# Six gate units made in pairs by seven block products, in the state space projections' stage

## The chip, the cores and the metric

The kernel runs on one core of one Trainium2 chip. The metric is the device time of one execution in microseconds (us). A measurement is the median of three runs; the profile is one more execution, recorded by the hardware.

## The reference, cut to what matters

One decoder layer over 1024 tokens with 1024 channels, in float32. Three mixers read one input projection, and each one's output is weighted by gates from the same projection:

```python
h = rms_norm(x, pre_mix_norm)
proj = h @ w_in
z, xbc, dt_raw, sb_qkv, nsa_q, nsa_kv, nsa_gate, merge_gate = split(proj)
y_ssm = ssm_mixer(z, xbc, dt_raw, ...)
y_sb  = stick_breaking_attention(sb_qkv)
y_nsa = nsa_attention(nsa_q, nsa_kv, nsa_gate, ...)
gm = sigmoid(merge_gate).reshape(bsz, s, 3, D_MODEL)
mixed = gm[:, :, 0] * (y_ssm @ w_br_ssm) + gm[:, :, 1] * (y_sb @ w_br_sb) + gm[:, :, 2] * (y_nsa @ w_br_nsa)
x = x + rms_norm(mixed @ w_out, post_mix_norm)      # then a convolved, gated feed-forward layer

def stick_breaking_attention(q, k, v):              # 4 heads of 128; for each block of queries
    ls = log_sigmoid(q @ k.T * scale)
    lk = where(mask, ls - q @ k.T * scale, 0)
    later = cumsum(lk, reversed over the keys) - lk # a sum that runs from the last key to the first
    out = where(mask, exp(ls + later), 0) @ v
```

The merge gates are 3072 channels, 24 units of 128 channels. The change concerns six of these units.

## The kernel before, in words

Everything is held with channels on the partitions and tokens along the free dimension. A float32 operand of TensorE is split into a high part (a copy in a shorter format) and a low part (the difference), and a product is made as three matmuls, high x high, high x low and low x high, of 128 x 128 weights by 128 x 512 tokens.

**A unit** is 128 output channels for all 1024 tokens. Made directly (`fine_steps`, `half_unit`), it is two halves of 512 tokens, each of 8 steps of 3 matmuls: 48 matmuls. ScalarE makes the high part of the weights (`whi`, L287), GpSimd the low part (`wlo`, L292). A gate unit ends with `sigmoid` (L262 to L264: Exp, Ln, Exp on ScalarE) and a DMA to a scratch tensor `g_d` (L580).

**The state space projections' stage** (`ssm_units`, from about 65 to 330 us) makes 24 units in 12 pairs. A pair is a 2 x 2 block product (two units by two token halves, with the depth in two halves) made with seven block products in place of eight. `weights7` (L532 to L552) loads both units' weights, forms the sums of blocks on GpSimd and splits them; `product` issues the 12 matmuls of one block product; `snap` (L610) copies a partial sum out of PSUM on ScalarE, and VectorE combines. A convolution (L325 to L331) and Silu (L622) follow, in a table set of ScalarE of its own; Exp and Ln are in another, and the program switches between them with table loads. One gate unit (number 0) is made directly ahead of the pairs.

**The sparse attention's stage** (to about 800 us) takes gate units 1 to 11 as filling between its own matmuls.

**The stick-breaking attention's stage** (`sb_stage`, about 820 to 1145 us) goes over four heads. A head has two chains, `chain(h, 1, ...)` for the later 512 queries, with eight blocks of 128 keys, and `chain(h, 0, ...)` for the earlier 512, with four. Each block of keys is a round of three steps:
- `score`: three matmuls into a bank of `ps_s` (or `ps_t` for chain 0); then VectorE takes a minimum (L1196), ScalarE Exp and Ln (L1197, L1198) and a copy (L1200), VectorE a maximum (L1201) and on the diagonal a mask (L1185).
- `carry`: VectorE subtracts the running sum's row of the round before (L1211), ScalarE makes `s_hi` (L1214), GpSimd `s_lo` (L1215), and two matmuls with a triangle (`rtab`) follow in the same bank.
- `value`: VectorE adds the bank to the copy (L1223), ScalarE takes Exp (L1224) and `w_hi` (L1228), VectorE `w_lo` (L1229), and three matmuls with the values go to `ps_o` (or `ps_b`).

Two banks are there for `ps_s`, so a score two rounds on waits for the addition L1223 that empties its bank.

Between these steps `fill.take` hands out steps of filling, `SB_FILL` per step of a chain on average: first the projections of the next head (three direct units, 144 matmuls, and some transposes), then the gate units `SB_GATES[h]` to `SB_GATES[h+1]`. Heads 0, 1 and 2 have two gate units each, head 3 has four (18 to 21), and two more (22, 23) are held back behind the last head's end.

**What sets the order.** The order of the instructions of each engine is fixed when the program is built, by a list scheduler that takes an instruction from later in the program where the next one's operands aren't ready by its own clock (`schedule_with_timeline_sim=True`). In the sparse attention's stage TensorE keeps the written order. On the chip each engine works through its fixed list in order. Tiles of one pool are handed out in the written order, so a unit that waits for a buffer holds back the ones behind it.

Of the kernel before, what the change touches and what calls it, by code (L numbers as in the profile page):

```python
# [28 lines left out]
PV_PRE, PV_FFN, PV_SSM, PV_D, PV_CW, PV_CB, PV_FW, PV_FB, PV_PM, PV_PF = np.cumsum(  # L29
    [0, 8, 8, 8, 8, 64, 16, 132, 44, 8]).tolist()  # L30
# [139 lines left out]

START_GATES = 1
N_GATES = 12
SB_GATES = (12, 14, 16, 18, 22, 24)

SB_LATE = 24

# [4 lines left out]
NSA_LEAD = 0  # L181
NSA_SWITCH = (10, 1)
MM_LAG = 3
SB_FILL = (2.2, 2.2, 2.2, 2)

SSD_AT = (0, 1, 8, 9)

# [23 lines left out]
def trunk(ctx: ExitStack, tc: tile.TileContext, A: dict, outT: bass.AP, dbg=None):  # L211
    nc = tc.nc
    act = nc.scalar.activation
# [18 lines left out]
    TABLE = "natural_log_exp_and_others"  # L232
# [28 lines left out]
    def sigmoid(dst, src):  # L261
        act(dst, src, AF.Exp, scale=-1.0)  # L262
        act(dst, dst, AF.Ln, bias=1.0)
# [55 lines left out]
    def hs(h):  # L319
        return slice(h * 512, (h + 1) * 512)  # L320

    def conv(o, h, ps, taps, bias, halo):

        n = len(taps) - 1
        act(o, ps, AF.Identity, bias=bias, scale=taps[0])  # L325
        if h == 0:
            V.tensor_copy(halo[:, :n], ps[:, 512 - n:])
        for d in range(1, n + 1):
            V.scalar_tensor_tensor(o[:, d:], ps[:, :512 - d], taps[d], o[:, d:], op0=OP.mult, op1=OP.add)  # L329
            if h == 1:  # L330
                V.scalar_tensor_tensor(o[:, :d], halo[:, n - d:n], taps[d], o[:, :d], op0=OP.mult, op1=OP.add)  # L331
# [240 lines left out]

    gp = hx.enter_context(tc.tile_pool(name="gp", reuse_waits="tile", bufs=2))

    def gates(j0, j1, steps=unit_steps):
        for j in range(j0, j1):
            def evict(h, ps):
                e = gp.tile([128, 512], F32, name="gate_e")
                sigmoid(e, ps)
                nc.sync.dma_start(g_d[j * 128:(j + 1) * 128, hs(h)], e)  # L580
            yield from steps(U_GATE + j, evict)
# [4 lines left out]
    def ssm_units():  # L586


        wx = early.enter_context(tc.tile_pool(name="wx0", side="right", reuse_waits="tile", bufs=2))
        ev = early.enter_context(tc.tile_pool(name="ev", side="right", reuse_waits="tile", bufs=2))  # L590
        rhs = {q: [None] * 4 for q in range(1, 8)}
        for k in range(4):
            b = [xs[h][k + n] for n in (0, 4) for h in range(2)]
            combos(*b, V)
            for q, n, h in ((1, 0, 0), (2, 4, 0), (3, 4, 1)):
                rhs[q][k] = h_rhs(k + n, h)
            for q, t in zip((6, 5, 4, 7), b):
                rhs[q][k] = t
        for q in (6, 7, 5, 4):
            for k in range(4):  # L600
                t, hi, lo = rhs[q][k], x_t(), x_t()
                act(hi, t, AF.Copy)
                V.tensor_tensor(lo, t, fl(hi), op=OP.subtract)
                rhs[q][k] = hi, lo

        Fill(gates(0, START_GATES)).rest()

        def snap(ps):
            t = x_t(F32)
            act(t, ps, AF.Copy)  # L610
            return t

        for q, m in itertools.product(range(4), (0, 2, 1)):
            u0 = 6 * q + 2 * m
            halos = [ev.tile([128, 4], F32, name="halo", bufs=4) for _ in range(2)]

            def evict(n, h, ps):
                o = ev.tile([128, 512], F32, name="o")
                if m < 2:
                    cu = q * 4 + 2 * m + n  # L620
                    conv(o, h, ps, [pvc(PV_CW, 4 * cu + 3 - d) for d in range(4)], pvc(PV_CB, cu), halos[n])
                act(o, o if m < 2 else ps, AF.Silu)  # L622
                nc.sync.dma_start(s_d[(u0 + n) * 128:(u0 + n + 1) * 128, hs(h)], o)

            w = weights7(wx, A["wfm"][U_SSM + u0], A["wfm"][U_SSM + u0 + 1], 512)
            x, y, z, v = ps_d(), ps_s(), ps_t(), (ps_o, ps_b)[m % 2]()
            product(x, w, rhs, 1, True)
            s1 = snap(x)
            product(y, w, rhs, 2, True)
            V.tensor_tensor(y, y, s1, op=OP.add)  # L630
            evict(0, 0, y)
            product(x, w, rhs, 6, False)
            s2 = snap(x)
            product(z, w, rhs, 7, True)
            product(x, w, rhs, 5, False)
# [1275 lines left out]
```

## Time and profile before

| | |
|---|---|
| time, median of 3 runs | 2241.54 us (2239.26 to 2242.5) |
| the profiled execution, first to last instruction | 2244.0 us |
| TensorE busy | 2167.6 us, 97% of the span |
| VectorE, ScalarE, GpSimd busy | 1314.7, 1204.4, 1269.3 us |
| first and last carry of the longer chains, stick-breaking stage | 841.99 us and 1142.53 us |

The profiled execution has no other time of its own than this span, which is 2.5 us above the median. A matmul of 512 columns shows as 0.39 us, but matmuls overlap, and in an undisturbed stretch one starts every 0.22 us; time for TensorE is therefore counted below by starts. Below, "lost" is time in which TensorE starts nothing though the list has more.

### The profile page before, as it was taken

The numbers are of one execution on the slowest core, as the hardware profiler recorded it, in microseconds if no ns is written. First come the engines' busy times: TensorE is split into PE (matmuls) and PEld (weight loads), VectorE is DVE, ScalarE is ACT, GpSimd is POOL, SyncE is SP. The second block draws the span as 40 slices with busy tenths as digits, with TensorE's granted clock in tenths as the row PEclk, the third lists the DMA queues.
The fourth block names the chain that finished last, engine by engine and source line by source line (L and its number), as shares of the span: only waits on it lengthen the run. The fifth ranks groups of instructions, "written<-read, shape, count | busy, mean of one in ns | idle before, by whom it ended". The sixth has DMA issues, their size and how long they took to land.

```text
span 2244.0 us, 30112 instructions
## 1 busy us (share of the span) xinstructions
PE 2167.6 (97%) x10589; PEld 1731.7 (77%) x10589; DVE 1314.7 (59%) x2419; ACT 1204.4 (54%) x2240; POOL 1269.3 (57%) x1122
## 2 busy tenths in 40 slices
PE   7999999999999999999999999999999999999997
PEld 7888889876666688888776678888778888878887
DVE  6765545257557426556537662228955767675776
ACT  6544442467757746667755531236644444575534
POOL 3777641146746734333337646568686777765743
PEclk9999999999999999999999999999999999999999
DMA  5233341321221011112262264235332323255433
GB/s 174 82 113 108 113 134 55 111 84 35 55 75 34 13 57 41 64 59 88 99 216 87 81 219 141 88 128 184 116 99 80 118 94 113 99 187 175 141 104 118
DMA packets 120104, 234.64 MB, mean 105 GB/s; under 512 B 28816, under 2 KB 43088, under 8 KB 119952
## 3 DMA queue, kind: packets, MB, share of 16 engines
q1 hardware_dynamic: 117072, 230.13, 31.2%
q10 hardware_dynamic: 2880, 2.59, 0.3%
q8 instruction: 83, 1.36, 0.3%
q14 instruction: 69, 0.57, 0.1%
HBM read 169.10 MB, written 63.57 MB: 104 GB/s over the span
## 4 chain that ended last, share of the span: by engine, by line
PE 80%; DVE 6%; ACT 4%; POOL 3%; issue 3%; DMA 2%; SPq 0%; DVEq 0%; ACTq 0%; POOLq 0%
PE dense L219 55%; PE ps_s L219 7%; PE ps_o L219 7%; PE ps_t L219 6%; PE ps_b L219 4%; PE psn L219 3%; DVE u L329 1%; POOL wlo L292 1%; POOL wlo L538 0%; DMA wraw<-in_wfm 0%; ACT dec L1302 0%; ACT wT L1000 0%; DMA traw<-in_wtm 0%; POOL h_lo L472 0%; DVE x L1530 0%
## 5 line engine op out<-in xcount | busy, mean ns | idle before, releaser
L292 POOL TENSOR_TENSOR wlo<-wraw,whi 128x256 fp32r<-128x256 f32 x344 | 273.1, 825 | 274.3 <-ACT whi L287 274.1
L219 PE MATMUL dense<-h_hi,whi 128*128 128x512 f32 x656 | 262.6, 400 | 0.0
L219 PE MATMUL dense<-h_hi,wlo 128*128 128x512 f32 x656 | 256.7, 392 | 1.2 <-POOL wlo L538 1.2
L219 PE MATMUL dense<-h_lo,whi 128*128 128x512 f32 x656 | 256.5, 391 | 0.0
L1011 POOL TENSOR_TENSOR wT_lo<-wT,wT_hi 128x512 fp32r<-128x512 f32 x132 | 168.8, 1288 | 84.8 <-ACT wT_hi L1010 76.5
L219 PE MATMUL dense<-hi,whi 128*128 128x512 f32 x576 | 214.5, 391 | 1.3 <-ACT whi L287 1.3
L219 PE MATMUL dense<-hi,wlo 128*128 128x512 f32 x512 | 200.8, 394 | 0.5 <-POOL wlo L292 0.4
L219 PE MATMUL dense<-x,uhi 128*128 128x512 f32 x600 | 191.8, 392 | 2.7 <-ACT uhi L546 1.5
L219 PE MATMUL dense<-lo,whi 128*128 128x512 f32 x448 | 176.1, 393 | 0.0
L287 ACT ACTIVATE whi<-wraw 128x1024 fp32r<-128x1024 f32 (+1 forms) x94 | 92.6, 985 | 154.4 <-PE dense L219 125.3
L547 POOL TENSOR_TENSOR ulo<-uf,uhi 128x1024 fp32r<-128x1024 f32 x38 | 91.8, 2416 | 115.0 <-ACT uhi L546 109.6
L219 PEld LDWEIGHTS dense<-h_hi,wlo 128*128 128x128 f32 x656 | 123.1, 188 | 27.9 <-POOL wlo L538 1.6
L219 PEld LDWEIGHTS dense<-h_hi,whi 128*128 128x128 f32 x656 | 123.7, 189 | 23.4
L219 PEld LDWEIGHTS dense<-h_lo,whi 128*128 128x128 f32 x656 | 123.5, 188 | 22.7
L219 PEld LDWEIGHTS dense<-x,uhi 128*128 128x128 f32 x600 | 112.4, 188 | 28.4 <-ACT x L610 2.4
L1215 POOL TENSOR_TENSOR s_lo<-sa,s_hi 128x512 fp32r<-128x512 f32 (+2 forms) x48 | 53.7, 1119 | 139.7 <-ACT s_hi L1214 139.7
L219 PEld LDWEIGHTS dense<-hi,whi 128*128 128x128 f32 x576 | 108.4, 188 | 25.5 <-ACT whi L287 2.1
L972 DVE TENSOR_REDUCE mx<-ps_t 128x1 f32<-128x384 f32 (+3 forms) x192 | 98.7, 520 | 48.9 <-PE ps_t L219 46.0
L329 DVE SCALAR_TENSOR_TENSOR u<-dense,pv,u 128x511 f32<-128x511 f32 (+1 forms) x140 | 103.5, 741 | 34.5 <-ACT u L325 34.5
L219 PEld LDWEIGHTS dense<-hi,wlo 128*128 128x128 f32 x512 | 96.3, 188 | 23.7 <-POOL wlo L292 2.0
L550 POOL TENSOR_TENSOR ulo<-uf,uhi 128x1024 fp32r<-128x1024 f32 x38 | 91.8, 2415 | 39.6 <-ACT uhi L549 38.0
L538 POOL TENSOR_TENSOR wlo<-wraw,whi 128x1024 fp32r<-128x1024 f32 x38 | 92.8, 2441 | 30.2 <-ACT whi L537 30.1
(555 smaller groups left out, 6088.4 us busy)
## 6 DMA issues: line engine op xcount, KB each, us to landing
wraw<-in_wfm SPq DMA_DIRECT2D x62, 512.0 KB, 3.7
wraw<-in_wup SPq DMA_DIRECT2D x52, 512.0 KB, 3.5
lo<-m_d SPq DMA_DIRECT2D x58, 256.0 KB, 3.2
g_d<-gate_e SPq DMA_DIRECT2D x48, 256.0 KB, 2.0
s_d<-o SPq DMA_DIRECT2D x48, 256.0 KB, 2.0
ge<-g_d SPq DMA_DIRECT2D x24, 512.0 KB, 3.4
m_d<-u SPq DMA_DIRECT2D x44, 256.0 KB, 2.0
row<-s_d SPq DMA_DIRECT2D x16, 512.0 KB, 5.0
```

The source lines that it names most:

```text
L219: i = f(*a, **k)
L287: act(hi, raw, AF.Copy)
L292: (V if tiles else P).tensor_tensor(lo[:, s], raw[:, s], fl(hi[:, s]), op=OP.subtract)
L329: V.scalar_tensor_tensor(o[:, d:], ps[:, :512 - d], taps[d], o[:, d:], op0=OP.mult, op1=OP.add)
L538: P.tensor_tensor(wlo, raws[0], fl(whi), op=OP.subtract)
L547: P.tensor_tensor(l24, f24, fl(h24), op=OP.subtract)
L550: P.tensor_tensor(l31, f31, fl(h31), op=OP.subtract)
L972: V.tensor_reduce(mx[:, h, a, n:n + 1], pm[:, :w], axis=AX, op=OP.max)
L1011: P.tensor_tensor(lo, wf, fl(hi), op=OP.subtract)
L1215: (P if SB_SLO else V).tensor_tensor(s_lo[:, c0:], a[:, c0:], fl(s_hi[:, c0:]), op=OP.subtract)
```

## The change

Gate units 12 to 17 leave the filling of heads 0, 1 and 2 of the stick-breaking stage. They are made in the state space projections' stage as three pairs, by the same seven block products as the state space units, behind the last of those. The code of a pair becomes a function `pair(u, m, evict)`, and the end of a gate unit a function `gate_out`. The instruction that loads the table set with Exp and Ln is written a second time, between the state space pairs and the gate pairs. `SB_FILL`, the steps of filling per step of a chain, goes from 2.2 to 1.4 for heads 0 to 2, as the filling there goes from 80 to 48 steps a head. Heads 0 to 2 now have the next head's projections alone as filling; head 3 has its four gate units, and the two held back are as before.

```diff
 N_GATES = 12
-SB_GATES = (12, 14, 16, 18, 22, 24)
+PAIR_GATES = 12, 18
+SB_GATES = (18, 18, 18, 18, 22, 24)
...
-SB_FILL = (2.2, 2.2, 2.2, 2)
+SB_FILL = (1.4, 1.4, 1.4, 2)
...
+    def gate_out(j, h, ps):
+        e = gp.tile([128, 512], F32, name="gate_e")
+        sigmoid(e, ps)
+        nc.sync.dma_start(g_d[j * 128:(j + 1) * 128, hs(h)], e)
...
-        for q, m in itertools.product(range(4), (0, 2, 1)):
...
-            w = weights7(wx, A["wfm"][U_SSM + u0], A["wfm"][U_SSM + u0 + 1], 512)
+        def pair(u, m, evict):
+
+            w = weights7(wx, A["wfm"][u], A["wfm"][u + 1], 512)
             x, y, z, v = ps_d(), ps_s(), ps_t(), (ps_o, ps_b)[m % 2]()
             product(x, w, rhs, 1, True)
             s1 = snap(x)
...
+        for q, m in itertools.product(range(4), (0, 2, 1)):
...
+            pair(U_SSM + u0, m, evict)
+        tc.keep_in_program_order(nc.scalar.preload_act_table_set(TABLE))
+        for m, j in enumerate(range(*PAIR_GATES, 2)):
+            pair(U_GATE + j, m, lambda n, h, ps: gate_out(j + n, h, ps))
```

The rows below are from the lists that the scheduler made, one row an instruction: line, operation, output <- inputs, shape. Line numbers of the changed kernel are 1 to 25 higher than before (L220 for L219, L647 for L622).

**TensorE, the last head of the stick-breaking stage, chain 1.** `row` tiles are queries and keys, `s_hi` and `s_lo` the operands of a carry, `w_hi` and `w_lo` those of a value step, `dense` is filling. Before:

```order
L219 MATMUL ps_s<-row_10135,row_10137 128x512
L219 MATMUL ps_s<-s_hi,rtab 128x512
L219 MATMUL ps_s<-row_10136,row_10137 128x512
L219 MATMUL ps_s<-row_10135,row_10138 128x512
L219 MATMUL dense<-h_hi,whi 128x512
L219 MATMUL dense<-h_lo,whi 128x512
L219 MATMUL dense<-h_hi,wlo 128x512
L219 MATMUL ps_s<-s_lo,rtab 128x512
L219 MATMUL ps_t<-s_hi,rtab 128x384
```

And now:

```order
L220 MATMUL ps_s<-s_lo,rtab 128x512
L220 MATMUL ps_o<-w_hi,row_10295 128x384
L220 MATMUL ps_o<-w_hi,row_10296 128x384
L220 MATMUL ps_o<-w_lo,row_10295 128x384
L220 MATMUL ps_s<-row_10291,row_10293 128x512
L220 MATMUL ps_s<-row_10292,row_10293 128x512
L220 MATMUL ps_s<-row_10291,row_10294 128x512
L220 MATMUL ps_s<-s_hi,rtab 128x512
L220 MATMUL ps_s<-s_lo,rtab 128x512
L220 MATMUL ps_o<-w_hi,row_10295 128x512
```

Before, filling stands between the carries of this chain in all rounds but one; now the filling stands earlier in the list, and six rounds in a row of this head have none.

**TensorE, the end of chain 1 of the second head.** Before, the last rounds of it (`ps_o` with `row_8729`) have filling among them:

```order
L219 MATMUL ps_s<-s_lo,rtab 128x512
L219 MATMUL ps_s<-row_9430,row_9433 128x256
L219 MATMUL dense<-h_hi,whi 128x512
L219 MATMUL ps_o<-w_hi,row_8729 128x512
L219 MATMUL ps_o<-w_hi,row_8730 128x512
L219 MATMUL dense<-h_lo,whi 128x512
L219 MATMUL dense<-h_hi,wlo 128x512
L219 MATMUL ps_o<-w_lo,row_8729 128x512
```

And now (the same chain's `ps_o` has `row_9161`; `ps_t` is the next head's chain 0):

```order
L220 MATMUL ps_s<-row_9157,row_9160 128x512
L220 MATMUL ps_s<-s_hi,rtab 128x512
L220 MATMUL ps_o<-w_hi,row_9161 128x512
L220 MATMUL ps_o<-w_hi,row_9162 128x512
L220 MATMUL ps_s<-s_lo,rtab 128x512
L220 MATMUL ps_o<-w_lo,row_9161 128x512
L220 MATMUL ps_t<-s_hi,rtab 128x512
```

The gate units that stood between these rounds are gone, and the next head's projections stand ahead of them.

**ScalarE, the end of the state space units.** Before (`o` is the output of a state space unit, `thi` and `whi` belong to what follows):

```order
L622 ACTIVATE o<-o 128x512
L384 ACTIVATE thi<-traw 128x512 x2
L856 ACT_TABLE_LOAD
L856 ACTIVATE ea<-hv 128x16
L325 ACTIVATE o<-dense,pv 128x512
L622 ACT_TABLE_LOAD
```

And now (`uhi` are weights of the first gate pair):

```order
L647 ACTIVATE o<-o 128x512
L263 ACT_TABLE_LOAD
L263 ACTIVATE gate_e<-ps_s 128x512
L264 ACT_TABLE_LOAD
L264 ACTIVATE gate_e<-gate_e 128x512
L265 ACT_TABLE_LOAD
L265 ACTIVATE gate_e<-gate_e 128x512
L647 ACT_TABLE_LOAD
L647 ACTIVATE o<-o 128x512
L550 ACTIVATE uhi<-uf_2821 128x1024
```

The first gate half stands ahead of the last Silu: three loads for its three functions, one back to Silu's set, and one more behind it. From the first pair on there are five table loads here, where three were.

More of the change, by code (lines that the diff above doesn't have):

```diff
@@ L573, in trunk @@
     gp = hx.enter_context(tc.tile_pool(name="gp", reuse_waits="tile", bufs=2))
+    def gate_out(j, h, ps):
+        e = gp.tile([128, 512], F32, name="gate_e")
+        sigmoid(e, ps)
+        nc.sync.dma_start(g_d[j * 128:(j + 1) * 128, hs(h)], e)
     def gates(j0, j1, steps=unit_steps):
         for j in range(j0, j1):
[L577 to L581, printed above, removed]
+            yield from steps(U_GATE + j, lambda h, ps: gate_out(j, h, ps))
     s_d = scratch("s_d", [24 * 128, T])
@@ L611, in snap @@
             return t
-        for q, m in itertools.product(range(4), (0, 2, 1)):
[L614 to L623, printed above, removed]
-            w = weights7(wx, A["wfm"][U_SSM + u0], A["wfm"][U_SSM + u0 + 1], 512)
+        def pair(u, m, evict):
+            w = weights7(wx, A["wfm"][u], A["wfm"][u + 1], 512)
             x, y, z, v = ps_d(), ps_s(), ps_t(), (ps_o, ps_b)[m % 2]()
@@ L644, in ssm_units, with evict @@
             evict(0, 1, x)
+        for q, m in itertools.product(range(4), (0, 2, 1)):
+            u0 = 6 * q + 2 * m
+            halos = [ev.tile([128, 4], F32, name="halo", bufs=4) for _ in range(2)]
+            def evict(n, h, ps):
+                o = ev.tile([128, 512], F32, name="o")
+                if m < 2:
+                    cu = q * 4 + 2 * m + n
+                    conv(o, h, ps, [pvc(PV_CW, 4 * cu + 3 - d) for d in range(4)], pvc(PV_CB, cu), halos[n])
+                act(o, o if m < 2 else ps, AF.Silu)
+                nc.sync.dma_start(s_d[(u0 + n) * 128:(u0 + n + 1) * 128, hs(h)], o)
+            pair(U_SSM + u0, m, evict)
+        tc.keep_in_program_order(nc.scalar.preload_act_table_set(TABLE))
+        for m, j in enumerate(range(*PAIR_GATES, 2)):
+            pair(U_GATE + j, m, lambda n, h, ps: gate_out(j + n, h, ps))
     ssm_units()
-    tc.keep_in_program_order(nc.scalar.preload_act_table_set(TABLE))
     early.close()
```

## The prediction

> **What bounds the kernel now.** I read the page first: shares of the engines, and the chain that ended last.
>
> ```profile
> PE 2167.6 (97%) x10589; PEld 1731.7 (77%) x10589; DVE 1314.7 (59%) x2419; ACT 1204.4 (54%) x2240; POOL 1269.3 (57%) x1122
> PE 80%; DVE 6%; ACT 4%; POOL 3%; issue 3%; DMA 2%; SPq 0%; DVEq 0%; ACTq 0%; POOLq 0%
> ```
>
> TensorE (PE) bounds the whole, so a matmul less is worth its start interval, as long as the stage it leaves still keeps TensorE supplied. The interval comes from a stretch of the projections' stage, in the view by windows (length, then busy time and count of each engine, TensorE's clock, DMA):
>
> ```profile
> 120.00:140.00 20.00, 20.00 (x89) 16.39 (x88) 5.12 (x8) 8.06 (x12) 13.74 (x9) 1.00 0.43 145
> ```
>
> 89 matmuls in 20 us are 0.2247 us each. ScalarE is busy 8 and GpSimd 14 of the 20 us, so gate pairs have room there.
>
> The stage that gives the work up is different. Its longer chains are serial: each of 32 rounds needs the carry of the round before. In the timeline, the second matmul of a carry (start, duration) marks a round's end; here are the first of the 32, three near the end, and the last:
>
> ```profile
> 841.99 0.38 PE L219 MATMUL ps_s<-s_lo,rtab 128*128 128x256 f32 x1
> ...
> 1104.37 0.39 PE L219 MATMUL ps_s<-s_lo,rtab 128*128 128x512 f32 x1
> 1112.93 0.40 PE L219 MATMUL ps_s<-s_lo,rtab 128*128 128x512 f32 x1
> 1122.02 0.39 PE L219 MATMUL ps_s<-s_lo,rtab 128*128 128x512 f32 x1
> ...
> 1142.53 0.39 PE L219 MATMUL ps_s<-s_lo,rtab 128*128 128x512 f32 x1
> ```
>
> Counting TensorE's list between carries, a 512-wide matmul at 0.2247 us and a narrower one in proportion: the round to 1112.93 holds 8.37 us of matmuls and took 8.56, so it was bound by TensorE. The next holds no filling, 4.33 us of matmuls, and took 9.09: 4.8 us lost. All 31 intervals hold 283.8 us and took 300.5, so some 12 us more are lost in small pieces. The windows show the hole:
>
> ```profile
> 1110.00:1115.00 5.00, 4.34 (x21) 3.12 (x19) 4.65 (x9) 3.95 (x8) 2.42 (x2) 1.00 0.25 92
> 1115.00:1120.00 5.00, 3.26 (x14) 1.95 (x14) 4.33 (x9) 4.49 (x9) 0.16 (x1) 1.00 0.14 52
> ```
>
> **The change part by part.**
>
> *Matmuls.* Six direct units are 6 x 48 = 288; three pairs are 3 x 84 = 252. Saved: 36 x 0.2247 = 8.1 us. The stick-breaking stage gives up 64.7 us, the projections' stage gains 56.6.
>
> *The projections' stage.* Table loads on ScalarE rise from three to five in this place. Before, they stood with room around them:
>
> ```profile
> 321.25 1.28 ACT L856 ACT_TABLE_LOAD   x1
> 322.55 0.22 ACT L856 ACTIVATE ea<-hv 128x16 f32<-128x16 f32 x1
> 325.54 0.63 ACT L622 ACTIVATE o<-o 128x512 f32<-128x512 f32 x1 [0.68 <-DVE o L331]
> 295.12 1.06 ACT L546 ACTIVATE uhi<-uf 128x1024 fp32r<-128x1024 f32 x1 [0.38 <-PE dense L219]
> L262 ACT ACTIVATE gate_e<-dense x48: 576/587/601, 61.4 to 1155.9; 128x512 f32<-128x512 f32 x48
> L263 ACT ACTIVATE gate_e<-gate_e x48: 612/632/695, 62.1 to 1158.6; 128x512 f32<-128x512 f32 x48
> ```
>
> Now they are queued ahead of `uhi`, weights of the first gate pair, for which TensorE waits. After the pair's second block product ScalarE has: Exp 0.59, load 1.28, Ln 0.63, load 1.28, Exp 0.63, load 1.28, Silu 0.63, `uhi` 1.06 = 7.4 us, and an addition on VectorE ahead of it (0.69, below): 8.1. TensorE's list has 35 matmuls there, 7.9 us. So 0.2 us shows, 0.5 with the hand-overs; bounds 0, and 8.1 if none of that cover held. [...] Here the next instruction follows the load by 0.02 us, and the row decides.
>
> Of other waits, the snapshots' grow with three pairs more, and two gaps stand at the stage's end:
>
> ```profile
> PE dense L219 <- ACT x L610: 2.1, 4, 0.9
> 320.76 0.39 PE L219 MATMUL ps_t<-thi,h_hi 128*128 128x256 f32 x1 [0.59 <-ACT thi L384]
> 322.12 0.39 PE L219 MATMUL ps_t<-tlo,h_hi 128*128 128x256 f32 x1 [0.73 <-POOL tlo L385]
> ```
>
> 2.1 us over 12 pairs make 0.5 for three. The two gaps (1.3) may stay or go; I leave them. Projections' stage: +1.0 us. The sparse attention's list on TensorE is unchanged.
>
> *The stick-breaking stage.* Of its DMAs only the six units' weight loads and twelve stores go; they hid behind matmuls. What counts is the cover. In the changed list, rounds without filling (by the order, counted from 0) are 13 and 14 in the second head, with round 12 nearly bare, and 24 to 29 in the last head. Their matmuls: 5.56, 2.25, 1.80 = 9.6 us; and 2.36, 1.74, 2.19, 1.46, 1.63, 2.25 = 11.6 us. TensorE cannot run ahead, since its list is fixed and the next score waits for a bank. What does such a round cost? The trace has one link of it, from a score (PE) to the addition that frees a bank for the next:
>
> ```profile
> 1120.12 0.96 PE L219 MATMUL ps_s<-row,row 128*128 128x512 f32 x3
> 1121.19 0.69 DVE L1196 TENSOR_SCALAR sa<-ps_s 128x512 f32<-128x512 f32 x1 [0.52 <-PE ps_s L219]
> 1121.91 0.63 ACT L1197 ACTIVATE sa<-sa 128x512 f32<-128x512 f32 x1 [0.52 <-DVE sa L1196]
> 1122.52 0.60 ACT L1200 ACTIVATE sz<-ps_s 128x512 f32<-128x512 f32 x1
> 1123.01 0.62 ACT L1198 ACTIVATE sa<-sa 128x512 f32<-128x512 f32 x1
> 1123.66 0.69 DVE L1201 TENSOR_TENSOR sa<-ps_s,sa 128x512 f32<-128x512 f32 x1 [1.18 <-ACT sa L1198]
> 1124.46 0.68 DVE L1211 TENSOR_TENSOR sa<-sa,ps_s 1x512 f32<-1x512 f32 x1
> 1125.17 0.69 DVE L1223 TENSOR_TENSOR sz<-sz,ps_s 128x512 f32<-128x512 f32 x1
> ```
>
> 1125.86 - 1120.12 = 5.74 us. VectorE's changed list has these in this sequence in the bare rounds, so 5.74 is a round's period; the 9.09 is the upper bound, as in that round the shorter chain and a gate's sigmoid were in the way. Narrow rounds shrink as ScalarE's do:
>
> ```profile
> L1197 ACT ACTIVATE sa<-sa 128x512 f32<-128x512 f32 x24 | 15.1, 630 | 19.8 <-DVE sa L1196 19.8
> L1197 ACT ACTIVATE sa<-sa 128x384 f32<-128x384 f32 x8 | 4.2, 522 | 4.6 <-DVE sa L1196 4.5
> L1197 ACT ACTIVATE sa<-sa 128x256 f32<-128x256 f32 x16 | 6.7, 418 | 4.0 <-DVE sa L1196 4.0
> L1229 DVE TENSOR_TENSOR w_lo<-sz,w_hi 128x512 fp32r<-128x512 f32 x23 | 18.8, 820 | 21.4 <-ACT w_hi L1228 21.4
> ```
>
> By 522/630 and 418/630: 4.8 and 3.8 us. Second head: 3 x 5.74 - 9.6 = 7.6 lost. Last head: 2 x 3.8 + 4.8 + 3 x 5.74 = 29.6, less 11.6 = 18.0; the shorter chain's last four value steps share VectorE in rounds 24 to 26, about 4 us by their `w_lo`, additions and masks, of which I count half, 2. Together 27.6. Lost before and gone now: 4.8. Net +22.8. The floor is VectorE alone, 0.69 + 0.69 + 0.68 + 0.69 + 0.82 = 3.57 a wide round: 10.7 and 22.5 (with the narrow rounds in proportion at 2.4, 2.4 and 3.0, and the 4), so 1.1 + 10.9 lost, net +7.2. The ceiling is 9.09 a round, in proportion: 27.3 - 9.6 and 46.9 - 11.6, net +48.2.
>
> *The clock.* TensorE's clock drops after thin stretches:
>
> ```profile
> 524.00:526.00 2.00, 0.94 (x8) 0.40 (x7) 1.97 (x4) 1.25 (x3) 1.46 (x2) 1.00 0.27 74
> 526.00:528.00 2.00, 1.26 (x8) 0.50 (x7) 1.41 (x6) 0.63 (x1) 1.42 (x5) 1.00 0.00 0
> 528.00:530.00 2.00, 1.50 (x7) 1.21 (x8) 0.44 (x1) 0.24 (x1) 0.90 (x1) 0.62 0.02 4
> 530.00:532.00 2.00, 2.00 (x9) 1.39 (x7) 1.25 (x4) 1.25 (x3) 0.41 (x1) 0.53 0.15 45
> ```
>
> 2.2 us busy of 4 brought it to about half; 3.26 of 5 above did not. The bare rounds hold 39% (11.6 of 29.6). At half clock three score matmuls take 0.65 us more in a round's period: nine rounds 5.9, and one slow stretch of some 3.4 us behind each of two tails costs 1.7 each. Bounds 0 and 9.3; I take 4, since slow matmuls raise the busy share again. [...]
>
> *Sum:* -8.1 + 1.0 + 22.8 + 4 = +19.7 us: 2263.7 for the profile's 2244.0, and 2261 against the median 2241.54.
>
> **The rivals.**
> 1. *The saving stands*, because filling that moved ahead covers the 12 us of small losses elsewhere and bare rounds run at VectorE's floor: -8.1 + 1.0 + 7.2 - 12 = -11.9 at most, half of the 12 giving -5.9: 2236. For it: VectorE is the busiest engine in the hole. Against it: 5.74 had little beside it. Faster.
> 2. *Floor without that cover*: -8.1 + 1.0 + 7.2 = +0.1, 2242: no change.
> 3. *Bare rounds cost as the one of before did*, every engine's queue in the way: -8.1 + 1.0 + 48.2 + 4 = +45.1 at most; midway between the two periods, +32: 2274. For it: the only complete bare round measured. Against: no gates' sigmoids are left there in the second head.
> 4. *The table loads stall the pairs*: 8.1 us in place of 0.5, 2269 with the forecast's rest.
>
> **How the numbers follow.** What can be told from no change is 0.2%, 4.5 us. Forecast (slower by 8 to 28 us) 0.62; rival 3 0.13; rival 4 0.03; rival 2 0.09; rival 1 0.13. Faster 0.13, same 0.09, slower 0.78. The range runs from just under rival 2 to a little above rival 3's middle, 2240 to 2278; the forecast's own is 2250 to 2270.
>
> **What would show it.** In the changed profile TensorE should have holes of about 7 and 18 to 22 us ahead of the ends of the second and the last head, with waits for `sz` (L1223's addition) and `s_lo`, carries 5 to 6 us apart there, and clocks below 1.00; the projections' stage should end 57 us later with no hole over 2 us. A carry spacing of 3.6 us in the bare rounds, or small losses gone elsewhere, would make the forecast wrong on the fast side; 8 us or more on the slow side.

## The result, and the profile after

The changed kernel takes 2273.15 us (median; 2272.03 to 2278.21), the kernel before beside it 2242.02 us (2239.26 to 2243.87): a ratio of 1.0147, 95% interval 1.0135 to 1.0159. It is slower by 31 us, where 19.7 were forecast. The profiled execution's span is 2271.9 us, 27.9 more than that of before. In the table of experiments below, "before, value step first" leaves out two of its ten runs, which took 3068 and 3071 us at a clock of 0.65.

One sentence on the change has to be put right first: the table load for Exp and Ln is not written a second time but moved, from behind the state space units to the place between them and the gate pairs.

The page of the changed kernel, shares of the engines:

```profile
PE 2179.9 (96%) x10553; PEld 1736.1 (76%) x10553; DVE 1325.0 (58%) x2431; ACT 1218.4 (54%) x2257; POOL 1290.5 (57%) x1122
```

TensorE has 36 matmuls fewer and is busy 12.3 us longer. This is the first hint: the matmuls left were slower ones. The mean granted clock of TensorE in this execution is 0.981; in that of before it was 0.993.

The ends of the longer chains' rounds, in TensorE's timeline (start, duration; as for before): the first, the rounds at the end of the second head, those at the end of the last head, and the last.

```profile
905.16 0.39 PE L220 MATMUL ps_s<-s_lo,rtab 128*128 128x256 f32 x1
...
1010.28 0.39 PE L220 MATMUL ps_s<-s_lo,rtab 128*128 128x512 f32 x1
1020.45 0.63 PE L220 MATMUL ps_s<-s_lo,rtab 128*128 128x512 f32 x1
1026.40 0.63 PE L220 MATMUL ps_s<-s_lo,rtab 128*128 128x512 f32 x1
1032.94 0.63 PE L220 MATMUL ps_s<-s_lo,rtab 128*128 128x512 f32 x1
...
1114.39 0.39 PE L220 MATMUL ps_s<-s_lo,rtab 128*128 128x512 f32 x1
1120.90 0.38 PE L220 MATMUL ps_s<-s_lo,rtab 128*128 128x256 f32 x1 [0.30 <-POOL s_lo L1223]
1123.45 0.28 PE L220 MATMUL ps_s<-s_lo,rtab 128*128 128x256 f32 x1
1129.12 0.52 PE L220 MATMUL ps_s<-s_lo,rtab 128*128 128x384 f32 x1
1135.61 0.63 PE L220 MATMUL ps_s<-s_lo,rtab 128*128 128x512 f32 x1
1142.00 0.63 PE L220 MATMUL ps_s<-s_lo,rtab 128*128 128x512 f32 x1
1149.40 0.63 PE L220 MATMUL ps_s<-s_lo,rtab 128*128 128x512 f32 x1
...
1170.71 0.39 PE L220 MATMUL ps_s<-s_lo,rtab 128*128 128x512 f32 x1
```

Three numbers split the 27.9 us of the spans:
- The first carry comes 63.2 us later than before (905.16 against 841.99). Of these, 56.6 are the matmuls that the projections' stage gained, and 6.6 are lost ahead of this carry.
- The 31 intervals take 265.55 us where they took 300.5: 35 us won for 64.7 us of matmuls given up. They hold 219.06 us of matmuls (counted in TensorE's list, as for before), so 46.5 us are lost in place of 16.7: 29.8 more.
- From the last carry to the end of the span it is 1101.2 us against 1101.5. Nothing is won or lost there.

So 6.6 + 29.8 - 8.1 = 28.3, which is the 27.9 but for the ends. The waits of TensorE between 850 and 1180 us (total, times, longest) name the place in the chains:

```profile
PE ps_s L220 <- DVE sz L1231: 13.9, 6, 3.0
PE ps_o L220 <- ACT w_hi L1236: 3.0, 2, 2.6
```

The next scores wait for the addition on VectorE that frees their bank. Here is one such round without filling in the last head, from one start of the scores to the next:

```profile
1127.59 1.42 PE L220 MATMUL ps_s<-row,row 128*128 128x512 f32 x3 [1.94 <-DVE sz L1231]
...
1129.12 0.69 DVE L1204 TENSOR_SCALAR sa<-ps_s 128x512 f32<-128x512 f32 x1 [0.24 <-PE ps_s L220]
...
1129.84 0.63 ACT L1205 ACTIVATE sa<-sa 128x512 f32<-128x512 f32 x1 [0.52 <-DVE sa L1204]
...
1130.85 0.62 ACT L1206 ACTIVATE sa<-sa 128x512 f32<-128x512 f32 x1
1131.50 0.69 DVE L1209 TENSOR_TENSOR sa<-ps_s,sa 128x512 f32<-128x512 f32 x1 [1.37 <-ACT sa L1206]
...
1132.55 0.54 DVE L1219 TENSOR_TENSOR sa<-sa,ps_s 1x384 f32<-1x384 f32 x1
1133.13 0.56 DVE L1231 TENSOR_TENSOR sz<-sz,ps_s 128x384 f32<-128x384 f32 x1
...
1133.74 1.65 PE L220 MATMUL ps_s<-row,row 128*128 128x512 f32 x3 [2.97 <-DVE sz L1231]
```

This is the ring of the forecast: scores, minimum, Exp, copy, Ln, maximum, (a mask,) row sum, addition. One turn is 6.15 us. The carry before had started its last matmul at 1129.12 (0.52 long), but the addition that reads it came only at 1133.13: it stands in VectorE's list behind the maximum, which waits for Ln.

### The profile page after: what moved, and what is told of

The parts are those of the page before. It is cut to its first block, busy times and chain, and to the rows that moved or that the text cites. A ratio compares the mean times of both kernels' runs of the same rounds, so it can differ in the third digit from the quotient of the medians.

```text
span 2271.9 us, 30095 instructions
## 1 busy us (share of the span) xinstructions
PE 2179.9 (96%) x10553; PEld 1736.1 (76%) x10553; DVE 1325.0 (58%) x2431; ACT 1218.4 (54%) x2257; POOL 1290.5 (57%) x1122
## 4 chain that ended last, share of the span: by engine, by line
PE 78%; DVE 7%; ACT 6%; POOL 3%; issue 3%; DMA 2%; SPq 0%; DVEq 0%; ACTq 0%; POOLq 0%
PE dense L220 52%; PE ps_s L220 7%; PE ps_o L220 7%; PE ps_t L220 6%; PE ps_b L220 4%; PE psn L220 2%; DVE u L330 1%; ACT h_hi L427 0%; ACT wT L1008 0%; DMA wraw<-in_wfm 0%; DVE x L1538 0%; POOL wlo L293 0%; POOL wlo L539 0%; POOL alo L553 0%; DVE sa L1219 0%
## 5 line engine op out<-in xcount | busy, mean ns | idle before, releaser
L293 POOL TENSOR_TENSOR wlo<-wraw,whi 128x256 fp32r<-128x256 f32 x320 | 254.6, 826 | 253.8 <-ACT whi L288 253.3
L220 PE MATMUL dense<-h_hi,whi 128*128 128x512 f32 x572 | 230.8, 404 | 1.1 <-ACT gate_e L263 0.7
L220 PE MATMUL dense<-h_hi,wlo 128*128 128x512 f32 x572 | 224.8, 393 | 1.2 <-POOL wlo L539 1.2
L220 PE MATMUL dense<-h_lo,whi 128*128 128x512 f32 x572 | 224.6, 393 | 0.0
L1019 POOL TENSOR_TENSOR wT_lo<-wT,wT_hi 128x512 fp32r<-128x512 f32 x132 | 168.7, 1287 | 83.5 <-ACT wT_hi L1018 76.0
L220 PE MATMUL dense<-hi,whi 128*128 128x512 f32 x576 | 214.7, 392 | 1.3 <-ACT whi L288 1.3
L220 PE MATMUL dense<-x,uhi 128*128 128x512 f32 x648 | 205.8, 390 | 2.9 <-ACT uhi L547 1.5
L220 PE MATMUL dense<-hi,wlo 128*128 128x512 f32 x512 | 201.2, 394 | 0.5 <-POOL wlo L293 0.4
L220 PE MATMUL dense<-lo,whi 128*128 128x512 f32 x448 | 176.6, 395 | 0.0
L288 ACT ACTIVATE whi<-wraw 128x1024 fp32r<-128x1024 f32 (+1 forms) x88 | 86.3, 981 | 153.1 <-PE dense L220 125.0
L548 POOL TENSOR_TENSOR ulo<-uf,uhi 128x1024 fp32r<-128x1024 f32 x41 | 98.9, 2413 | 121.5 <-ACT uhi L547 115.7
L220 PEld LDWEIGHTS dense<-x,uhi 128*128 128x128 f32 x648 | 121.3, 188 | 30.3 <-ACT x L612 2.4
L220 PEld LDWEIGHTS dense<-hi,whi 128*128 128x128 f32 x576 | 108.5, 188 | 25.4 <-ACT whi L288 2.1
L551 POOL TENSOR_TENSOR ulo<-uf,uhi 128x1024 fp32r<-128x1024 f32 x41 | 99.0, 2414 | 50.8 <-ACT uhi L550 48.9
L220 PEld LDWEIGHTS dense<-h_hi,wlo 128*128 128x128 f32 x572 | 107.8, 188 | 24.8 <-POOL wlo L539 1.6
L220 PEld LDWEIGHTS dense<-h_hi,whi 128*128 128x128 f32 x572 | 108.4, 190 | 22.6 <-ACT gate_e L263 1.1
L220 PEld LDWEIGHTS dense<-h_lo,whi 128*128 128x128 f32 x572 | 108.3, 189 | 20.3
L220 PEld LDWEIGHTS dense<-hi,wlo 128*128 128x128 f32 x512 | 96.5, 189 | 23.8 <-POOL wlo L293 2.0
```

The source lines that it names most:

```text
L220: i = f(*a, **k)
L288: act(hi, raw, AF.Copy)
L293: (V if tiles else P).tensor_tensor(lo[:, s], raw[:, s], fl(hi[:, s]), op=OP.subtract)
L548: P.tensor_tensor(l24, f24, fl(h24), op=OP.subtract)
L551: P.tensor_tensor(l31, f31, fl(h31), op=OP.subtract)
L1019: P.tensor_tensor(lo, wf, fl(hi), op=OP.subtract)
```

## The experiments

All ran on the chip in three rounds beside the kernel before, whose medians were 2240.74, 2241.07 and 2240.66 us in the three groups. Theories are named as in the expectations.

| kernel | time, us | ratio, 95% interval | 31 intervals, us |
|---|---|---|---|
| changed kernel | 2273.15 | 1.0135 to 1.0159 | 265.55 |
| pairs left out | 2208.69 | 0.9845 to 0.9874 | 265.88 |
| filling tied to the chains | 2270.63 | 1.0119 to 1.0153 | 264.53 |
| stores on another queue | 2273.03 | 1.0130 to 1.0161 | 265.32 |
| gate pairs first | 2267.75 | 1.0108 to 1.0138 | 265.75 |
| value step first | 2273.51 | 1.0134 to 1.0170 | 265.18 |
| before, value step first | 2240.96 | 0.9993 to 1.0013 | 298.65 |
| both of these edits | 2267.22 | 1.0105 to 1.0135 | 265.13 |
| both, one pair only | 2241.91 | 0.9995 to 1.0014 | 283.75 |
| row copied out | 2285.16 | 1.0183 to 1.0217 | 272.31 |
| minimum three times | 2311.66 | 1.0287 to 1.0332 | 302.55 |
| before, minimum three times | 2271.44 | 1.0121 to 1.0152 | 329.72 |
| `s_lo` twice | 2280.63 | 1.0161 to 1.0191 | 270.53 |

### The two stages apart: the pairs left out

```diff
-        for m, j in enumerate(range(*PAIR_GATES, 2)):
-            pair(U_GATE + j, m, lambda n, h, ps: gate_out(j + n, h, ps))
+        half = gp.tile([128, 512], F32, name="gate_e")
+        V.memset(half, 0.5)
+        for j in range(*PAIR_GATES):
+            for h in range(2):
+                nc.sync.dma_start(g_d[j * 128:(j + 1) * 128, hs(h)], half)
```

> The changed kernel without the three pairs: the six gate units are not computed (a constant 0.5 stands in their place), so the output lacks them; the stick-breaking stage is that of the change. Theory (rounds without filling lose the time, whatever comes ahead): 64.7 us of matmuls go and about 30 us are lost, so 2242 - 35 = 2207 us (2202 to 2212). Rival (the loss comes from what the pairs leave behind): without pairs nothing is lost, 2242 - 65 = 2177 us.

Measured: 2208.69 us, 32.05 below the kernel before. The theory holds. This splits the result by times, without a profile: the stick-breaking stage gave up 64.7 us of matmuls and the kernel became 32.05 us shorter, so 32.65 are lost there. The three pairs then cost 31.13 + 32.05 = 63.2 us for 56.6 us of matmuls, so 6.6 are lost by the pairs, the same as the first carry showed. That the figure agrees to a tenth is luck: the 32.65 here and the 29.8 of the profiles are 2.9 apart.

### Is it where the filling stands? Filling tied to the chains

```diff
-                fill.take(int(m))
+                with tc.issue_after(last[0].ins) if last[0] else nullcontext():
+                    fill.take(int(m))
```

> The change, with each step's filling tied behind the last value step's matmul, so that the scheduler cannot move it ahead. The same matmuls, SB_GATES and SB_FILL; by TensorE's list no wide round has fewer than 4.8 us of matmuls but one (2.9), and one narrow one has 2.2. Theory (period of 5.74 us a bare round, and the clock): the nine bare rounds lost 36 us, the thin ones here lose about 7, so 2273 - 29 = 2244 us (2240 to 2254). Rival (the stage as a whole has too little work beside its chains, 8.2 us a round being the chains' own pace): 2268 to 2274 us wherever the filling stands.

Measured: 2270.63 us. The theory falls. In TensorE's list hardly a round is bare now (most hold 5 to 9 us of matmuls), and the 31 intervals are still 264.53 us. Most rounds with 4.8 to 6.5 us of matmuls take 7.0 to 8.0. The timeline of one shows what filling does to the ring; `L288` makes high parts of the filling's weights, `L1147` is an eviction of the filling:

```profile
1051.86 0.85 PE L220 MATMUL ps_s<-row,row 128*128 128x512 f32 x3
...
1052.81 0.69 DVE L1204 TENSOR_SCALAR sa<-ps_s 128x512 f32<-128x512 f32 x1 [1.53 <-PE ps_s L220]
...
1053.54 0.63 ACT L1205 ACTIVATE sa<-sa 128x512 f32<-128x512 f32 x1 [2.71 <-DVE sa L1204]
...
1054.56 1.05 ACT L288 ACTIVATE whi<-wraw 128x1024 fp32r<-128x1024 f32 x1
...
1055.50 0.62 ACT L1206 ACTIVATE sa<-sa 128x512 f32<-128x512 f32 x1
...
1056.16 0.69 DVE L1209 TENSOR_TENSOR sa<-ps_s,sa 128x512 f32<-128x512 f32 x1 [2.65 <-ACT sa L1206]
...
1056.76 0.68 DVE L1147 SCALAR_TENSOR_TENSOR row<-dense,row 128x512 fp32r<-128x512 f32 x1
...
1058.56 0.55 DVE L1231 TENSOR_TENSOR sz<-sz,ps_s 128x384 f32<-128x384 f32 x1
...
1059.17 1.24 PE L220 MATMUL ps_s<-row,row 128*128 128x512 f32 x3 [2.11 <-DVE sz L1231]
```

One turn is 7.31 us, 1.16 more than in the bare round, though the scores ran at full rate here (0.85 us for three against 1.42). The filling keeps TensorE busy, but its own steps on ScalarE (1.05 us between Exp and Ln) and VectorE (0.68 us between maximum and addition) stand in the ring. For this round that is read off the rows; that the other filled rounds go the same way is inferred from their length: 23 of the 31 intervals are under 10 us and make 165 us, 7.2 each, for 142 us of matmuls. The other eight, at and beside the changes of heads, make 99 us for 76; what they wait for was not followed up, and they are half of the loss (23 of 46). The clock differs too: over the 31 intervals it was 0.97 here, 0.92 in the changed kernel and 1.00 before. The half clock alone doesn't make the length, then, since with less of it the stage is as long.

### The loss in the projections' stage: stores, and place of the pairs

TensorE's hole there, in two-microsecond windows (columns as before; PE busy is the second number, the clock the third from the end), and the rows around it:

```profile
342.00:344.00 2.00, 0.89 (x4) 0.39 (x3) 0.00 (x0) 0.53 (x1) 0.00 (x0) 1.00 0.12 49
344.00:346.00 2.00, 1.21 (x4) 0.73 (x5) 0.00 (x0) 2.00 (x5) 1.67 (x2) 1.00 0.00 0
346.00:348.00 2.00, 2.00 (x7) 1.56 (x6) 0.70 (x1) 1.97 (x5) 2.00 (x1) 0.56 0.02 4
348.00:350.00 2.00, 2.00 (x7) 1.53 (x6) 0.70 (x1) 1.97 (x4) 1.30 (x3) 0.59 0.35 131
```

```profile
330.08 1.04 ACT L550 ACTIVATE uhi<-uf 128x1024 fp32r<-128x1024 f32 x1
...
331.20 2.40 POOL L551 TENSOR_TENSOR ulo<-uf,uhi 128x1024 fp32r<-128x1024 f32 x1 [6.29 <-ACT uhi L550]
...
337.55 1.29 POOL L546 TENSOR_TENSOR uf<-uf,wraw 128x512 f32<-128x512 f32 x1
...
338.87 0.33 SPq L533 DMA_DIRECT2D wraw<-in_wfm  x1
...
343.48 0.63 ACT L552 ACTIVATE ahi<-wraw 128x512 fp32r<-128x512 f32 x1 [5.21 <-DMA wraw<-in_wfm]
...
344.01 0.58 ACT L263 ACTIVATE gate_e<-ps_o 128x512 f32<-128x512 f32 x1
...
344.64 0.73 PE L220 MATMUL ps_o<-x,ahi 128*128 128x512 f32 x2 [1.75 <-ACT gate_e L263]
```

`uhi` stands behind the table loads on ScalarE. GpSimd had been idle 6.29 us for it, so its sums of weight blocks ended late (338.84), and the next weights were requested at 338.87, right behind those sums. They came for `ahi` at 343.48; the first function of the sigmoid, which frees the bank `ps_o`, stands behind `ahi` on ScalarE. TensorE stood 1.75 us and then ran at 0.56 to 0.59 of its clock for some 4 us. This is not all of the 6.6 us: TensorE's waits for the snapshots (`x`, L612) between 60 and 400 us grew from 2.1 to 3.9, and a second wait for a sigmoid is 0.7. The half clock is no net loss in this pair of traces, since before had such a stretch too, at 528 us, that is gone here. The rest was not followed up.

A first suspicion was the store queue, since SP had spent 7.12 us on two stores just ahead of those weights:

```diff
-                nc.sync.dma_start(s_d[(u0 + n) * 128:(u0 + n + 1) * 128, hs(h)], o)
+                (nc.scalar if u0 == 20 else nc.sync).dma_start(s_d[(u0 + n) * 128:(u0 + n + 1) * 128, hs(h)], o)
```

> The change, with the last state space pair's four stores issued from ScalarE's queue, not SyncE's. Theory (the third pair's weight load waited behind such a store on SyncE's queue, which waited for the last Silu): the load comes earlier, the hole of 2.1 us near 343 us and the half clock behind it go, 2273 - 4 = 2269 us. Rival (ScalarE's own queue, with table loads and sigmoids, makes the hole): 2272 to 2275 us.

Measured: 2273.03 us, no gain. The wait for the bank was still 1.7 us, and the weights were requested at 338.70. The stores were not what was late. Next, the gate pairs were put ahead of the state space pairs, away from these table loads:

```diff
+        for m, j in enumerate(range(*PAIR_GATES, 2)):
+            pair(U_GATE + j, m, lambda n, h, ps: gate_out(j + n, h, ps))
         for q, m in itertools.product(range(4), (0, 2, 1)):
...
         tc.keep_in_program_order(nc.scalar.preload_act_table_set(TABLE))
-        for m, j in enumerate(range(*PAIR_GATES, 2)):
-            pair(U_GATE + j, m, lambda n, h, ps: gate_out(j + n, h, ps))
```

> The change, with the three gate pairs ahead of the state space pairs, where the table set with Exp and Ln is still loaded. Theory (the 6.6 us lost in the projections' stage come from the pairs standing behind the last Silu: table loads, a held-up weight load): 5 us come back, 2268 us. Rival (the pairs themselves overload ScalarE, wherever they stand, or the stage's beginning, where VectorE and GpSimd are over 90% busy, has no room): 2272 to 2278 us.

Measured: 2267.75 us, 5.4 less than the changed kernel, as expected (4.1 if each is set against the kernel before beside it). The windows of 300 to 400 us, of the changed kernel and then of this one, show the hole gone:

```profile
300.00:400.00 100.00, 95.34 (x424) 76.96 (x422) 32.42 (x60) 54.61 (x82) 55.22 (x45) 0.98 0.36 121
```

```profile
300.00:400.00 100.00, 98.46 (x454) 80.75 (x452) 52.85 (x99) 45.60 (x65) 56.46 (x45) 1.00 0.40 127
```

The same move on top of the next section's edit ("value step first" against "both of these edits" in the table) is worth 6.3. So some 4 to 6 of the 6.6 us hang on the place of the pairs. That it is the table loads ahead of `uhi`, and no other neighbour of that place, is what the rows say; it wasn't tried by itself.

### What sets the pace of a bare round? Four tries

The addition that frees the bank stands in VectorE's list behind the maximum. In the next kernel the value step is written ahead of the carry step:

```diff
-            for f, m in ((carry, n - 1), (value, n - 2), (score, n)):
+            for f, m in ((value, n - 2), (carry, n - 1), (score, n)):
```

> The change as it is, with one edit in the stick-breaking chains: in each round the value step of the block before last is written ahead of the carry step of the last block, so that on VectorE the sum on sz (which gives a bank of ps_s back to the next scores) mostly stands ahead of the maximum on sa, which waits for ScalarE's Ln. All work is the same. In the changed kernel the next scores waited 13.9 us in all for that sum, and a thin round took 6.39 us (6.15 of it from one start of the scores to the next, of which some 3.5 are the wait of the sum behind the maximum). Theory (the bank of ps_s that comes back late, behind the maximum in VectorE's order, sets the pace of the thin rounds): the nine thin rounds fall from about 6.4 to about 5 us, the stage from 265.6 to 250-258 us, the kernel from 2273 to 2258-2266 us, and the wait of ps_s for sz falls below 6 us. Rival (the chain of one block after another through ScalarE, GpSimd and TensorE sets the pace, whatever stands first in VectorE's order): the stage stays at 263-268 us and the kernel at 2270-2276 us.

Measured: 2273.51 us. The theory's time falls, and the rival's holds. But the wait had not gone; it had another name:

```profile
PE ps_s L220 <- DVE sa L1219: 5.8, 3, 3.0
```

```profile
1137.92 0.69 DVE L1231 TENSOR_TENSOR sz<-sz,ps_s 128x512 f32<-128x512 f32 x1 [1.37 <-PE ps_s L220]
1138.53 0.68 DVE L1209 TENSOR_TENSOR sa<-ps_s,sa 128x512 f32<-128x512 f32 x1
...
1139.25 0.68 DVE L1219 TENSOR_TENSOR sa<-sa,ps_s 1x512 f32<-1x512 f32 x1
...
1139.98 0.73 PE L220 MATMUL ps_s<-row,row 128*128 128x512 f32 x2 [2.09 <-DVE sa L1219]
```

The row sum also reads the bank, and it too stands behind the maximum. Ahead of the maximum the addition now stands, and it waited 1.37 us for the carry's matmuls; the maximum, though Ln had ended at 1138.22, stood behind it. So in this round the carry's own chain is the ring: from one row sum (1133.59) through `s_hi`, `s_lo`, the carry's matmuls, addition and maximum to the next (1139.25) it is 5.66 us. The next ring is only half a microsecond shorter than the one that was opened, which is the rival's mechanism. And the 31 intervals were 265.18 us in all, so other rounds took longer.

> The kernel before with the same one edit in the chains (value step written ahead of carry step), nothing else. The kernel before lost 16.7 us in these rounds beside 283.8 us of matmul work. Theory (bank of ps_s late, but covered by filling there): at most a few us, 2234-2242 us. Rival of before (its rounds too are set by the chains' order): 2225-2232 us.

Measured on the kernel before: 2240.96 us, no change, inside the theory's 2234 to 2242.

So the row that the row sum needs was copied out of the bank by VectorE ahead of the maximum, on top of the last edit:

```diff
-                V.tensor_tensor(row, row, st[kb + 1][0][0:1, b0:], op=OP.subtract)
+                V.tensor_tensor(row, row, st[kb + 1][-1][:, b0:], op=OP.subtract)
...
             mm(pz[:, c0:], E.neg_tri_r, s_lo[:, c0:], start=False, stop=True)
+            out = pz[0:1]
+            if c and kb:
+                out = wk.tile([128, 512], F32, name="ysb", bufs=2)[SWAP[0]:SWAP[0] + 1]
+                V.tensor_copy(out[:, c0:], pz[0:1, c0:])
+            st[kb] = pz, a, z, out
```

> The kernel with the value step written first, and one thing more: in the longer chains VectorE copies the one row that a carry hands on out of the bank (1x512, about 0.6 us) right behind the carry's matmuls, and the next block's row sum reads the copy. With the value step first the next scores waited for that row sum (VectorE, on sa, 5.8 us in all), since it is the last reader of the bank and stands behind the maximum; the copy lets the bank go ahead of the maximum. Theory (the bank that comes back behind the maximum sets the pace of the thin rounds; the first edit only swapped one last reader for another): a thin round falls from about 5.7-6.5 to 4.5-5 us, the stage from 265 to 253-260 us, the kernel to 2260-2268 us, and no wait of ps_s for sa or sz of over 3 us is left. Rival (the links of the chain one after another set the pace whatever frees the bank): 2270-2277 us, the waits only pass to another name.

Measured: 2285.16 us, slower than either side expected. The wait passed back to the addition (9.6 us in all). One round of the last head shows how:

```profile
1143.86 0.68 DVE L1230 COPY ysb<-ps_s 1x512 f32<-1x512 f32 x1 [1.71 <-PE ps_s L220]
1144.58 0.69 DVE L1209 TENSOR_TENSOR sa<-ps_s,sa 128x512 f32<-128x512 f32 x1
1145.18 0.68 DVE L1236 TENSOR_TENSOR sz<-sz,ps_s 128x512 f32<-128x512 f32 x1
...
1145.92 1.65 PE L220 MATMUL ps_s<-row,row 128*128 128x512 f32 x3 [2.09 <-DVE sz L1236]
```

The copy waited for the carry's matmuls, the maximum waited behind the copy though Ln had ended at 1143.82, and the addition came behind both. The copy is now a link itself: VectorE is busy 189.5 us in the 31 intervals where it was 168.7. Letting the bank go by another reader doesn't help, then, as long as that reader too stands behind a late link in VectorE's fixed list. A list in which it doesn't was not tried.

The last two kernels make a link longer, one that is in the ring and one that is not, without other work:

```diff
-            V.tensor_scalar(a[:, c0:], pz[:, c0:], 60.0, None, op0=OP.min)
+            for _ in range(3 if c else 1):
+                V.tensor_scalar(a[:, c0:], pz[:, c0:], 60.0, None, op0=OP.min)
```

> The change with one link of the longer chains made longer without other work: VectorE takes the minimum of the scores three times instead of once (0.69 us each, 1.38 us more a round), with the same result. Theory (a thin round is a ring of scores, minimum, Exp, Ln, maximum and row sum, in which every link counts; filling hides it elsewhere, but is used up earlier since each round takes more of it): by the order's matmul work of each round and a thin round of 6.39 + 1.38 us, 25 us more, 2290-2305 us. Rival 1 (the sum of the work of the engines sets the stage): at most 5 us more, 2270-2279 us. Rival 2 (every round goes at the chains' pace): 31 times 1.38 = 43 us more, 2310-2320 us.

```diff
-            (P if SB_SLO else V).tensor_tensor(s_lo[:, c0:], a[:, c0:], fl(s_hi[:, c0:]), op=OP.subtract)
+            for _ in range(2 if c else 1):
+                (P if SB_SLO else V).tensor_tensor(s_lo[:, c0:], a[:, c0:], fl(s_hi[:, c0:]), op=OP.subtract)
```

> The change with another link longer: GpSimd makes the rest s_lo of the carry twice in the longer chains (1.28 us more a round), with the same result. In the trace of the changed kernel's thin rounds the carry's matmuls ended some 3.5 us before VectorE came to the sum on sz that follows them, so this link is not in the ring. Theory (only the ring of scores, minimum, Exp, Ln, maximum and row sum counts): at most 4 us more, 2270-2278 us. Rival (the carries one after another set the pace): 9 thin rounds times 1.28 = 11.5 us more at least, 2284 us or over.

Measured: with the minimum three times 2311.66 us, 38.5 more than the changed kernel; its 31 intervals are 37.0 us longer, 1.19 a round of the 1.38 at most that was added. With `s_lo` twice 2280.63 us, 7.5 more; the intervals are 5.0 longer, 0.16 a round of 1.28. The difference between the two links is the clearest reading of all: in the changed kernel's order the ring of the forecast counts nearly in full, the carry's own chain hardly. Both expectations had the direction and missed the size. The minimum's theory had counted on filling to hide the link outside bare rounds (25 us); rival 2, all rounds at the chains' pace, has the time in its range (2310 to 2320). The waits of the scores for the addition went from 13.9 us to this:

```profile
PE ps_s L220 <- DVE sz L1232: 31.2, 9, 5.3
```

One caution belongs here: the scheduler saw the longer link as well and spread the filling over fewer rounds, so that eleven rounds hold under 4 us of matmuls in place of eight. That the filling is used up earlier is part of the 37 us. The same in the kernel before:

> The kernel before with the same longer link. Theory: the filling of the kernel before only just covered the rounds; with each round 1.38 us longer it is used up about five rounds before the end, and the kernel loses as much as the changed one does, 15-28 us, 2256-2270 us. Rival (there the filling hides the link): 2239-2247 us.

Measured: 2271.44 us, 30.8 more than the kernel before beside it, a little over the theory's 15 to 28. There too the filling ran out: five rounds near the end (25 to 29) hold under 2.3 us of matmuls each. With 283.8 us of matmuls in its intervals, the kernel before had little reserve: its filling covered the chains and hardly more.

### How much can be taken away? Both edits, and one pair only

> The change with both edits: the three gate pairs ahead of the state space pairs (which alone took it to 2267.8 us), and the value step written ahead of the carry step. Theory: the two gains are in different stages and add: about 5.4 us below the kernel that has the value step first alone, 2252-2261 us. Rival: the second edit gives nothing, 2265-2270 us.

Measured: 2267.22 us, as with the pairs first alone (2267.75). Of the two gains, one is nothing. With this as a base, one pair in place of three:

```diff
-PAIR_GATES = 12, 18
-SB_GATES = (18, 18, 18, 18, 22, 24)
+PAIR_GATES = 12, 14
+SB_GATES = (14, 15, 16, 18, 22, 24)
-SB_FILL = (1.4, 1.4, 1.4, 2)
+SB_FILL = (1.8, 1.8, 2.2, 2)
```

> As the kernel with both edits, but only gate units 12 and 13 are made as a pair; 14 stands in head 0's filling, 15 in head 1's, 16 and 17 in head 2's, with rates 1.8, 1.8, 2.2 and 2. TensorE's work in the 31 rounds is then about 265 us instead of 222 with three pairs and 284-286 with none, and the matmuls saved are 2.7 us instead of 8.1. Theory (what is lost comes from rounds with too little work beside the chains, and grows with each pair taken away): the stage loses 18-25 us, the kernel takes 2236-2247 us, between the kernel before with the value step first and three pairs. Rival (the stage's length is the chains' own, about 250-265 us, so that one pair comes out free): 2225-2235 us, below the kernel before.

Measured: 2241.91 us, the same as the kernel before (0.9995 to 1.0014), inside the theory's range. The 31 intervals hold 264.9 us of matmuls and take 283.75, so 18.8 are lost. The kernels to set this against have the value step first too: before lost 12.7 in this order (285.9 us of matmuls in 298.65), three pairs lose 43.5 (221.7 in 265.13). The first pair's 21 us less in these rounds thus bring 14.9; the next two's 43.2 less bring 18.6. But the pair's first carry came 24.9 us later than in the kernel before with the value step first (865.69 against 840.75) for 18.9 us of matmuls, with 5.8 us of TensorE waiting for the snapshots (`x`, L612) between 60 and 400 us, where the changed kernel has 3.9. That is 6.0 us lost ahead of the chains, more than the 2.7 saved. No version beat the kernel before.

## Why the prediction was right, and where it was too small

The direction and the place were right. By the prediction's steps:

- **Matmuls, -8.1.** Right: 36 fewer in the list.
- **The projections' stage, +1.0.** Measured +6.6. The price was worked out for the first gate pair's `uhi` alone, and there it was right: TensorE's list ran on until 342.9. What the step left out is the next thing that `uhi` makes late: GpSimd's sums, behind them the weights of a later pair, behind these the bank. The hole came 13 us after the last of the four loads in a row. The snapshots' waits, put at +0.5, grew by 1.8. Its upper bound of 8.1 held. The loads cost what the forecast's row has: 1.28 us each, and the row behind the last of the four starts at 329.54 for a load at 328.25, 0.01 us behind its end.
- **The stick-breaking stage, +22.8, and its clock, +4.** Together 26.8; measured +29.8 in the profiles, +32.65 by times. The bare rounds were the ones named, and the loss sits in them:

| round | matmuls, us | forecast, us | measured, us |
|---|---|---|---|
| 12 | 5.56 | 5.74 | 10.17 |
| 13, 14 | 2.25, 1.80 | 5.74 each | 5.95, 6.54 |
| 24, 25, 26 | 2.36, 1.74, 2.19 | 3.8, 3.8, 4.8 | 6.51, 2.55, 5.67 |
| 27, 28, 29 | 1.46, 1.63, 2.25 | 5.74 each | 6.49, 6.39, 7.40 |

The nine rounds take 57.7 us and lose 36.4, where 27.6 and 4 for the clock make 31.6. The ring was sized well: 5.74 plus 0.65 for three scores at half clock is 6.39, and rounds 27 and 28 took 6.49 and 6.39 (three scores take 1.65 us at 1133.74, where the forecast's row has 0.96). The clock term was given as 4 for the whole stage; the carries of seven rounds show 0.52 to 0.63 us where 0.28 to 0.39 is the full rate. Its slow stretch of 3.4 us is the one of the forecast's rows at 528 (0.62 and 0.53 over two windows of 2 us make 3.4 us at 0.50); the changed kernel's clock was 0.50 for 17.1 us from 1018.67 and for 23.9 us from 1127.89. The step that was mis-sized most is round 12, "nearly bare", taken at 5.74: with steps of both chains and the last of the filling in it, and a wait of 2.6 us for `w_hi`, it took 10.17, which is 4.4 of the 4.8 us missing. That the net came nearer is in part luck: the forecast took off 4.8 us for before's bare round alone, but before lost about 8.5 in these nine rounds (2.3 of it in round 13). They add about 28, then, where 26.8 were forecast. The other 22 rounds lose about 10.1 where they lost 8.2.
- **Rival 1**, that filling moved ahead covers small losses: nothing of its 12 shows. Outside the nine rounds about 2 us more are lost, not less.
- **Rival 3**, a bare round at 9.09: refuted for the five wide bare rounds behind round 12 (5.95 to 7.40), though its midway time, 2274, is by chance the nearest figure.
- **Rival 4**, the table loads stall the pairs: its mechanism is the one that the rows show in the projections' stage, one step further down the line than it said; that it is the loads was not tried by itself.

The forecast's reason, that rounds go bare because the filling stands earlier in the list, was half of the truth. The tied filling shows that no bare rounds are needed for the loss: with filling in nearly every round the stage is 264.5 us all the same. What the stage has too little of is work beside a ring that needs 6.15 us bare and 7.3 when the filling's own ScalarE and VectorE steps stand in it; the 7.3 is read off one round. Of the two orders tried, each lost the same; that none is better isn't shown.

## What to carry to other kernels

Before work is moved out from beside a chain of dependent steps, find the ring (here the time from one use of a bank to the next) and what a turn of it takes: cover is worth its full time only in the rounds that hold more work than that. Filling is not free cover, since what it does on the engines of the ring is a link too. Before opening a ring, look for the next one: here it was half a microsecond shorter. And where an instruction becomes late, follow it past its first reader: the loss may come two engines and 13 us later.

## What the runs showed of the hardware that was not expected

- The same hole brought the clock down in some traces and not in others. In the windows above, 2.10 us busy in the four from 342 were followed by 0.56 and 0.59, and the changed kernel's mean from 300 to 400 us is 0.98. With the stores on another queue TensorE waited 1.7 us for the same sigmoid, and the value step first changes nothing ahead of the chains; the mean clock of both is 1.00 there (stores, then value step first):

```profile
300.00:400.00 100.00, 95.77 (x436) 77.39 (x435) 32.65 (x61) 54.83 (x85) 54.76 (x44) 1.00 0.38 124
```

```profile
300.00:400.00 100.00, 95.55 (x436) 77.52 (x435) 32.54 (x61) 54.92 (x85) 54.82 (x44) 1.00 0.37 124
```

  TensorE's busy time in the four us ahead doesn't tell the cases apart, so the forecast's 2.2 us of four is no limit. In the changed kernel 2.36 us from 362 left the clock at 1.00; in the kernel before it fell at 692.32 us behind 2.65 us (the changed kernel, then the one before):

```profile
362.00:366.00 4.00, 2.36 (x11) 1.65 (x10) 1.19 (x3) 3.62 (x7) 2.81 (x3) 1.00 0.56 182
366.00:370.00 4.00, 4.00 (x19) 3.26 (x18) 0.38 (x1) 3.81 (x7) 1.94 (x2) 1.00 0.55 211
```

```profile
688.32:692.32 4.00, 2.65 (x18) 1.66 (x16) 2.72 (x9) 4.00 (x13) 3.53 (x4) 1.00 0.63 197
692.32:695.32 3.00, 3.00 (x10) 2.01 (x9) 1.94 (x6) 0.44 (x2) 2.72 (x5) 0.50 0.00 0
```

  What decides it was not shown.

- The place of an event moved by 4 us between two profiles, with the clock. The first carry came at 901.11 us with the pairs first and at 905.14 with both edits, though the second edit touches nothing ahead of the chains and TensorE was busy 98.46 and 98.45 us between 300 and 400 in the two. With both edits the granted clock was 0.83 from 580 to 600 us and 0.91 from 660 to 680; with the pairs first it was 1.00 in both. That is 5.2 us' worth of clock. A term of 4 us or less is better taken from a difference of medians, as with the pairs left out, than from one place in two traces.
